# Which engine turns the normalised activations: K-tiles 8 to 15 on VectorE and through DRAM in place of TensorE

## The chip, the cores and the metric

The kernel runs on one core of one Trainium2 chip. It is a single launch, and its time is the device time of that launch in microseconds (us), given as the median of several runs. The engines that matter are TensorE (PE in the profile; its weight loads are shown apart as PEld), VectorE (DVE), ScalarE (ACT) and SyncE (SP), whose queue issues nearly all DMAs, one after the other. GpSimd (POOL) does almost nothing here.

## The reference

Two decoder layers on one sequence of 512 tokens and width 2048, all in float32. Layer 0 is a differential attention, layer 1 a forgetting attention that reads keys, values and forget gates projected once from the output of layer 0. The place of the change is the seam between the two: the layer norm that ends layer 0 and the projection behind it.

```python
def layer_norm(x, g, b):
    mu = jnp.mean(xf, axis=-1, keepdims=True)
    var = jnp.mean(jnp.square(xf - mu), axis=-1, keepdims=True)
    return (xf - mu) * lax.rsqrt(var + EPS) * g + b
...
y = diff_attention(h, ...)                       # ends in  o @ w_out
x = layer_norm(DN_ALPHA * x + gate * y, ln_g[0], ln_b[0])
...
# shared_kv
hk = x * (1.0 + scale) + shift
kvf = hk @ w_kv                                  # 2048 -> 4096 + 16
...
# layer 1
h = x * (1.0 + scale) + shift                    # another scale and shift
proj = h @ w_q                                   # 2048 -> 4096
```

## The kernel before

**Arithmetic.** Every float32 product is done as three products of rounded parts: an operand is split into a high part (`Hh`, `whi`) and the rest (`Hl`, `wlo`), and `products` (lines 227 to 231) issues high x high, high x low and low x high into one PSUM bank. The left or right operand on the activations' side has to lie with the width of 2048 on the partitions, so it is kept as 16 K-tiles of 128 features x 512 tokens, `Hh[kt]` and `Hl[kt]`.

**Weights.** `WeightStream` (lines 73 to 162) loads weights by SP's queue into four stage tiles (`wst`); each is cast by ACT into `whi` (line 117), DVE takes the rest into `wlo` (line 118), three buffers each.

**The end of layer 0.** `out_projection(oA, 0, ...)` multiplies by `a_w_out` in four jobs of 512 columns (f = 0 to 3). In the last job the weights of the last five of eight K-pairs are held back (`hold=5`, line 1089), and then worked off token block by token block (b = 0 to 3, 128 tokens each), five bursts of six matmuls a block. So block 0 is finished first. Behind each block comes `evac` on DVE (lines 1075 to 1086): the gate, the residual and the statistics, and then `norm_a(b)` (lines 1123 to 1130): mean and reciprocal deviation by a chain of small DVE instructions, the first 1024 columns of `n[:, b]` normalised by ACT, the others by DVE, and one store of the 1 MB block to `n_dram`, which layer 1 reads for its residual. `norm_a(3)` is the last of them.

**Turning.** `n` holds tokens on the partitions. `build_half(s, half)` (lines 1132 to 1153) makes one unit, K-tiles 2s and 2s + 1 for the token blocks 2 x half and 2 x half + 1: four TensorE transposes (line 1140) into a PSUM bank `sc`, of which there are two; for each K-tile two ACT instructions that apply scale and shift, into `htmp2` and into `Hh` (lines 1148 and 1149); one DVE subtraction into `Hl` (line 1150); and a DVE copy of the turned bank back over the same columns of `n` (line 1153). From there `build_h` (lines 1174 to 1180) later makes the `Hh` and `Hl` of layer 1 with the other scale and shift.

**The joint.** The first job on `kv_w` (`vj[0]`, 512 of the value columns) does not go K-pair by K-pair over all tokens but in the order `lag` (lines 1156 to 1159), 16 units written as (half, s): (0,0) (0,1) (0,2) (0,3) (1,0) (1,1) (1,2), then (0,s) (1,s-1) for s = 4 to 7, then (1,7). Half 0 runs ahead since token blocks 2 and 3 are normalised later. A unit consumes 12 matmuls of 512 columns (lines 1254 to 1258). `build_next` makes the next unit in that order: two are made during the last block of `out_projection` (line 1171), then one in each step of the loop (lines 1245 to 1262) except step 2, so that from step 3 on a unit is built one step ahead of its matmuls. Behind each step of half 1 the weight stream goes one on. I number steps and units from 0.

The instructions are traced in the order of the code, and the framework then orders those of each engine by its own plan; `tc.keep_in_program_order` holds an instruction at its place in the code.

Of the kernel before, what the change touches and what calls it, by code (L numbers as in the profile page):

```python
# [10 lines left out]
F32 = mybir.dt.float32  # L11
F32R = mybir.dt.float32r
I32 = mybir.dt.int32
AF = mybir.ActivationFunctionType
ALU = mybir.AluOpType

P = 128
D = 2048
# [147 lines left out]
def tile_yoco(  # L166
# [23 lines left out]
    nc = tc.nc  # L190
    V, S, PE, G = nc.vector, nc.scalar, nc.tensor, nc.gpsimd
    PSUM = bass.MemoryType.PSUM

    x = x[0]
    out = out[0]
# [7 lines left out]
    dram = ctx.enter_context(tc.tile_pool(name="dram", bufs=1, space=bass.MemoryType.DRAM))  # L203

    n_dram = dram.tile([T, D], F32, name="n_dram")
# [5 lines left out]
    def acc_bank(name="acc"):  # L211
        return ps.tile([P, 512], F32, name=name, tag="acc", bufs=4)

    def sc_bank(name="sc"):
        return ps.tile([P, 512], F32, name=name, tag="sc", bufs=2)
# [7 lines left out]
    def split(hi, lo, src):  # L223
        S.copy(hi, src)
        V.tensor_tensor(lo, src, hi.bitcast(F32), op=ALU.subtract)

    def products(dst, lhs, rhs, start, stop):

        PE.matmul(dst, lhs[0], rhs[0], start=start, stop=False)  # L229
        PE.matmul(dst, lhs[0], rhs[1], start=False, stop=False)  # L230
        PE.matmul(dst, lhs[1], rhs[0], start=False, stop=stop)  # L231
# [9 lines left out]
        out=mask[:, 384:], in_=mask[:, 384:], compare_op=ALU.is_ge, fill=NEG, base=0, pattern=[[-1, P]],  # L241
# [85 lines left out]
    oA = [(f, Job(a_w_out, [(512 * f, 512)]), (0, 1, 2, 3)) for f in range(4)]  # L327
# [24 lines left out]
    Hh = [None] * KT  # L352
    Hl = [None] * KT

    def new_h(kt):
        Hh[kt] = hpool.tile([P, T], F32R, name="hh", tag="H")
        Hl[kt] = hpool.tile([P, T], F32R, name="hl", tag="H")
# [591 lines left out]
    def drain():  # L949
        while pieces:  # L950
            tick(0)
# [84 lines left out]
    def ktile(name):  # L1036
        return kpool.tile([P, T], F32, name=name, tag="K")


    def row_bcast(t, src):  # L1040
        nc.sync.dma_start(t, src.partition_broadcast(P))

    def moments(pool, stats, b):
        mv = pool.tile([P, 2], F32, name="mv", tag="mv", bufs=4)
        V.bn_aggr(mv, stats[:, b, :, :])
        ve = pool.tile([P, 1], F32, name="lve", tag="lve", bufs=4)
        rstd = pool.tile([P, 1], F32, name="lrstd", tag="lrstd", bufs=4)
        V.tensor_scalar(ve, mv[:, 1:2], EPS, None, op0=ALU.add)
        rsqrt(rstd, ve, 1, pool)
        return mv, rstd  # L1050

    def out_projection(jobs, layer, zp, opened, residual, norm, after_held=None):


        ready = {}

        def prepare(k):
            if k < len(jobs):
                ready[k] = residual(jobs[k][0], jobs[k][2])

        prepare(0)
        for k, (f, job, banks) in enumerate(jobs):
            if layer == 1:

                if k == 1:
                    for piece in later:
                        pieces.extend([None, None, piece])
                pieces.extend([None] * (8 if k > 1 else 0) + [lambda k=k: prepare(k + 1)])
            elif k:
                prepare(k)  # L1070
            res = ready[k]
            gate = ktile("gate")
            row_bcast(gate, gate_dram[layer][0, 512 * f : 512 * (f + 1)])

            def evac(b, acc, f=f, res=res, gate=gate):
                if f == 0 and b == 0:
                    drain()
                    opened()
                pool, z, stats = zp
                zs = z[:, b, 512 * f : 512 * (f + 1)]  # L1080
                tmp = pool.tile([P, 512], F32, name="ztmp", tag="htmp", bufs=2)
                V.tensor_tensor(tmp, acc, gate, op=ALU.mult)
                res(b, zs, tmp)
                V.bn_stats(stats[:, b, f, :], zs)
                if f == 3:
                    norm(b)

            last = k == len(jobs) - 1
            group(job, True, evac, banks, bg=1 if k == 0 and layer == 0 else 0, hold=(5, 6)[layer] if last else 0, after_held=after_held if last else None)

    nctx = ExitStack()
    zp = []

    ab = {}
# [18 lines left out]
    def fold(k, row):  # L1113
        nc.sync.dma_start(row[0 : 2 * KT, 0:P], mod_dram[k].rearrange("v (a p) -> (v a) p", p=P))
        pt = tr_bank()
        PE.transpose(pt[:, 0 : 2 * KT], row[0 : 2 * KT, 0:P], ident[0 : 2 * KT, 0 : 2 * KT])
        a1, b1 = cols(f"mod_a{k}"), cols(f"mod_b{k}")
        V.tensor_tensor(b1, pt[:, KT : 2 * KT], bncol, op=ALU.mult)
        V.tensor_tensor(b1, pt[:, 0:KT], b1, op=ALU.add)
        V.tensor_tensor(a1, pt[:, KT : 2 * KT], gcol, op=ALU.mult)  # L1120
        return a1, b1

    def norm_a(b):
        pool, n, stats = zp
        mv, rstd = moments(pool, stats, b)
        mr = pool.tile([P, 1], F32, name="mr", tag="mr", bufs=4)
        V.scalar_tensor_tensor(mr, mv[:, 0:1], -1.0, rstd, op0=ALU.mult, op1=ALU.mult)
        S.activation(n[:, b, 0:1024], n[:, b, 0:1024], AF.Identity, scale=rstd, bias=mr)
        V.tensor_scalar(n[:, b, 1024:], n[:, b, 1024:], mv[:, 0:1], rstd, op0=ALU.subtract, op1=ALU.mult)
        nc.sync.dma_start(n_dram[b * P : (b + 1) * P, :], n[:, b, :])  # L1130

    def build_half(s, half):

        pool, n, _ = zp
        px = sc_bank()
        hs = slice(256 * half, 256 * half + 256)
        for q in range(2):
            for b in range(2):
                src = n[:, 2 * half + b, (2 * s + q) * P : (2 * s + q + 1) * P]
                PE.transpose(px[:, q * 256 + b * P : q * 256 + (b + 1) * P], src, ident)  # L1140
        for q in range(2):
            kt = 2 * s + q
            if half == 0:
                new_h(kt)
            tmp = pool.tile([P, 256], F32, name="htmp2", tag="htmp2", bufs=2)
            pq = px[:, q * 256 : (q + 1) * 256]
            sc, sh = ab["kv"][0][:, kt : kt + 1], ab["kv"][1][:, kt : kt + 1]
            S.activation(tmp, pq, AF.Identity, scale=sc, bias=sh)
            S.activation(Hh[kt][:, hs], pq, AF.Identity, scale=sc, bias=sh)
            V.tensor_tensor(Hl[kt][:, hs], tmp, Hh[kt][:, hs].bitcast(F32), op=ALU.subtract)  # L1150

        place = n[:, 2 * half : 2 * half + 2, 2 * s * P : (2 * s + 2) * P].rearrange("p b (q t) -> p q b t", t=P)
        V.tensor_copy(place, px.rearrange("p (q b t) -> p q b t", q=2, b=2))
# [8 lines left out]
    def build_next(n=1):  # L1162
        for _ in range(n):
            unit = next(built, None)
            if unit:
                build_half(unit[1], unit[0])
# [1 line left out]
    pieces.extend(attention_a(A_HEADS - 1, 1))  # L1168
    pieces.append(lambda: split_og((14, 15)))
    pieces.append(lambda: ab.update(kv=fold(0, ktile("mrow"))))  # L1170
    out_projection(oA, 0, zp, open_n, residual_a, norm_a, lambda b, k: build_next() if b == 3 and k < 2 else None)
    npool, n, nstats = zp

    def build_h(kts, ab):
        for kt in kts:
            new_h(kt)
            tmp = npool.tile([P, T], F32, name="htmp", tag="htmp", bufs=2)
            nt = n[:, :, kt * P : (kt + 1) * P]
            V.tensor_scalar(tmp.rearrange("p (b t) -> p b t", t=P), nt, ab[0][:, kt : kt + 1], ab[1][:, kt : kt + 1], op0=ALU.mult, op1=ALU.add)
            split(Hh[kt], Hl[kt], tmp)  # L1180


# [59 lines left out]

    acc = [acc_bank() for _ in range(TB)]
    held = {}
    for i, (half, s) in enumerate(lag):
        if i != 2:
            build_next()
        if (half, s) == (0, 3):
            ws.step(lambda: kpool.tile([P, 512], F32R, name="held", tag="K"))
            ws.load(ws.done + ws.STAGES - 1)  # L1250
        if half == 0:
            held[s] = ws.get(vj[0], s, 0)
        hi, lo = held[s]
        for b in (2 * half, 2 * half + 1):
            bs = slice(b * P, (b + 1) * P)
            for kq in range(2):
                kt = 2 * s + kq
                products(acc[b], (Hh[kt][:, bs], Hl[kt][:, bs]), (hi[kq], lo[kq]), kt == 0, kt == KT - 1)
            if s == KT // 2 - 1:
                evac_v(0)(b, acc[b])  # L1260
        if half == 1:
            ws.advance(ws.where[id(vj[0]), s] + 4)
# [310 lines left out]
```

## Time and profile before

| what | value |
|---|---|
| median of 3 runs | 1947.01 us (1946.09 to 1948.02) |
| the profiled execution: its time | 1948.57 us |
| its span, first to last instruction | 1946.7 us |
| TensorE clock granted, mean | 0.998 |
| PE busy from 0 to 60 us, 60 to 960 us | 40.68, 898.93 us |
| PE busy from 960 to 1035 us | 74.56 us |
| PE busy from 1900 to 1946.7 us | 34.27 us |
| GpSimd busy, whole span | 2.2 us |

All times inside the execution are counted from the start of the span. A busy time is a sum of instruction durations with overlaps taken out, so it says that an engine was occupied, not that the work could not have been shorter; for that one looks at the starts of successive instructions. "Idle before, releaser" is the time an engine stood still ahead of an instruction, and what ended it.

### The profile page before, as it was taken

How to read it: one execution, taken by the hardware profiler on the slowest of the kernel's cores; microseconds unless marked ns; L12 is line 12 of the kernel's file. 1: busy time of each engine (PE TensorE's matmuls, PEld its weight loads, DVE VectorE, ACT ScalarE, POOL GpSimd, SP SyncE). 2: the span in 40 equal slices, each digit the busy share in tenths (PEclk: the TensorE clock that was granted, in tenths of full speed). 3: DMA queues.
4: the chain of work that ended last, by engine and by line, in shares of the span. 5: the costliest groups of instructions: out<-in, count | busy, mean ns of one | idle time of the engine just before them, and what ended most of it. 6: DMA issues, size and time to landing. Idle time of an engine off the chain costs nothing.

```text
span 1946.7 us, 25419 instructions
## 1 busy us (share of the span) xinstructions
PE 1913.4 (98%) x8945; PEld 1611.4 (83%) x8945; DVE 1345.4 (69%) x2375; ACT 704.8 (36%) x1204; POOL 2.2 (0%) x10
## 2 busy tenths in 40 slices
PE   6999999999999999999999999999999999999997
PEld 4888888888888878888889998888888888888886
DVE  7995678877787778643575756565566666696657
ACT  3333434323333325531273222224334344453123
POOL 0000000000000000000000000000000000000000
PEclk9999999999999999999999999999999999999999
DMA  9993566877878774353337867654355555557622
GB/s 336 382 325 93 162 221 205 255 252 235 256 236 262 227 247 157 121 168 98 130 122 235 290 200 231 224 184 130 110 152 151 151 153 158 146 161 228 193 93 102
DMA packets 311851, 378.75 MB, mean 195 GB/s; under 512 B 56838, under 2 KB 237340, under 8 KB 310956
## 3 DMA queue, kind: packets, MB, share of 16 engines
q1 hardware_dynamic: 308720, 372.90, 60.1%
q10 hardware_dynamic: 3004, 4.23, 0.6%
q8 instruction: 70, 1.15, 0.2%
q14 instruction: 57, 0.47, 0.1%
HBM read 346.94 MB, written 30.10 MB: 194 GB/s over the span
## 4 chain that ended last, share of the span: by engine, by line
PE 89%; DVE 5%; DMA 3%; issue 1%; ACT 1%; SPq 1%; DVEq 0%; ACTq 0%
PE acc L229 25%; PE acc L230 25%; PE acc L231 25%; PE acc L677 4%; PE sc L679 2%; PE o L229 1%; PE o L679 1%; PE o L231 1%; PE o L230 1%; PE sc L231 1%; PE sc L230 1%; PE sc L229 1%; DVE wlo L118 1%; DMA ms<-in_w_mod_dram 1%; DVE macc L457 1%
## 5 line engine op out<-in xcount | busy, mean ns | idle before, releaser
L118 DVE TENSOR_TENSOR wlo<-wst,whi 128x1024 fp32r<-128x1024 f32 (+2 forms) x298 | 351.3, 1179 | 326.0 <-ACT whi L117 320.3
L117 ACT CAST whi<-wst 128x1024 fp32r<-128x1024 f32 (+2 forms) x298 | 303.3, 1018 | 666.4 <-PE acc L231 321.8
L229 PE MATMUL acc<-hh,whi 128*128 128x512 f32 x1184 | 464.2, 392 | 0.8 <-DVE sg L774 0.8
L230 PE MATMUL acc<-hl,whi 128*128 128x512 f32 x1184 | 462.2, 390 | 0.0
L231 PE MATMUL acc<-hh,wlo 128*128 128x512 f32 x1184 | 461.8, 390 | 0.0
L229 PE MATMUL acc<-whi,hh 128*128 128x512 f32 (+1 forms) x1168 | 445.0, 381 | 0.0
L230 PE MATMUL acc<-wlo,hh 128*128 128x512 f32 (+1 forms) x1168 | 442.8, 379 | 0.3 <-DVE wlo L118 0.3
L231 PE MATMUL acc<-whi,hl 128*128 128x512 f32 (+1 forms) x1168 | 442.4, 379 | 0.0
L231 PEld LDWEIGHTS acc<-hh,wlo 128*128 128x128 f32 x1184 | 222.6, 188 | 47.3
L229 PEld LDWEIGHTS acc<-hh,whi 128*128 128x128 f32 x1184 | 222.7, 188 | 44.2 <-issue 1.8
L230 PEld LDWEIGHTS acc<-hl,whi 128*128 128x128 f32 x1184 | 222.8, 188 | 42.0
L231 PEld LDWEIGHTS acc<-whi,hl 128*128 128x128 f32 x1168 | 219.4, 188 | 35.7
L230 PEld LDWEIGHTS acc<-wlo,hh 128*128 128x128 f32 x1168 | 219.6, 188 | 34.2 <-DVE wlo L118 0.8
L229 PEld LDWEIGHTS acc<-whi,hh 128*128 128x128 f32 x1168 | 219.5, 188 | 34.1
L457 DVE SCALAR_TENSOR_TENSOR macc<-ms,cact,macc 128x1024 f32<-128x1024 f32 (+1 forms) x180 | 197.8, 1099 | 27.5 <-DMA ms<-in_kv_w_mod_dram 14.0
L568 DVE SCALAR_TENSOR_TENSOR sacc<-sms,cact,sacc 128x512 f32<-128x512 f32 x112 | 77.1, 746 | 4.8 <-DMA sms<-in_w_mod_dram 4.5
L804 ACT ACTIVATE e<-e,mn 128x128 f32<-128x128 f32 (+3 forms) x64 | 36.0, 563 | 102.6 <-DVE mn L800 100.3
L1375 ACT ACTIVATE eb<-eb,mnb 128x128 f32<-128x128 f32 (+1 forms) x64 | 36.0, 563 | 85.6 <-DVE mnb L1372 85.4
L677 PE MATMUL acc<-whi,hh 128*128 128x512 f32 x128 | 51.8, 408 | 0.0
L677 PE MATMUL acc<-wlo,hh 128*128 128x512 f32 x128 | 50.1, 392 | 0.8 <-DVE wlo L135 0.8
L126 ACT CAST whi<-wst 128x768 fp32r<-128x768 f32 (+1 forms) x30 | 28.3, 944 | 60.5 <-PE o L679 33.7
L677 PE MATMUL acc<-whi,hl 128*128 128x512 f32 x128 | 50.0, 390 | 0.0
(270 smaller groups left out, 1981.8 us busy)
## 6 DMA issues: line engine op xcount, KB each, us to landing
wst<-in_a_w_in_dram SPq DMA_DIRECT2D x237, 256.0 KB, 4.3
ms<-in_w_mod_dram SPq DMA_DIRECT2D x64, 512.0 KB, 4.5
ms<-in_kv_w_mod_dram SPq DMA_DIRECT2D x64, 512.0 KB, 4.3
sms<-in_w_mod_dram SPq DMA_DIRECT2D x56, 512.0 KB, 7.6
wst<-in_b_w_in_dram SPq DMA_DIRECT2D x112, 256.0 KB, 2.9
wst<-in_kv_w_dram SPq DMA_DIRECT2D x40, 512.0 KB, 3.7
wst<-in_a_w_out_dram SPq DMA_DIRECT2D x32, 512.0 KB, 3.7
msk<-in_w_mod_dram SPq DMA_DIRECT2D x64, 256.0 KB, 5.2
```

The costliest lines, as they stand in the source:

```text
L117: self.nc.scalar.copy(hi[:, :, :w], st[:, :, :w])
L118: self.nc.vector.tensor_tensor(lo[:, :, :w], st[:, :, :w], hi[:, :, :w].bitcast(F32), op=ALU.subtract)
L126: self.nc.scalar.copy(hi[:, :, : job.width], self.stage[self.done][:, :, : job.width])
L229: PE.matmul(dst, lhs[0], rhs[0], start=start, stop=False)
L230: PE.matmul(dst, lhs[0], rhs[1], start=False, stop=False)
L231: PE.matmul(dst, lhs[1], rhs[0], start=False, stop=stop)
L457: ins = V.scalar_tensor_tensor(acc, w, cact[:, kt : kt + 1], acc, op0=ALU.mult, op1=ALU.add)
L568: V.scalar_tensor_tensor(acc, w, sc, acc, op0=ALU.mult, op1=ALU.add)
L677: PE.matmul(bank(v, b), h[:, bs], w, start=start, stop=stop)
L679: PE.matmul(bank(v, b), w[:, bs], h, start=start, stop=stop)
L804: S.activation(e[:, :w], e[:, :w], AF.Exp, bias=mn, scale=-1.0, accum_out=rs)
L1375: S.activation(e[:, :w], e[:, :w], AF.Exp, bias=mn, scale=-1.0, accum_out=rs)
```

## The change

The units with s = 4 to 7, that is K-tiles 8 to 15 (columns 1024 to 2047 of `n`, two groups of 512 with f = 2 and f = 3), are no longer turned by TensorE.

- `turn_out(b, f)`: a DVE transpose of the 128 x 512 piece of `n`, which turns each 32 x 32 square, into a new tile `nturn` (three buffers), held in program order; then a 256 KB store into a DRAM tile.
- `bring(b, f)`: four loads of 64 KB from that DRAM tile back over the same piece of `n`, one for each group of 32 features; with them the squares come to the partitions where they belong.
- `far(kt, blocks)` is the view of such a piece that gives K-tile kt; `build_far` does the rest of a unit from it: the same four ACT instructions, now read from `n` in SBUF, and the same two DVE subtractions. There is no transpose, no PSUM bank and no copy.
- Where they stand: (0,2) and (0,3) are turned out during the held bursts of block 1, (1,2) and (1,3) during those of block 2, (2,2) at the end of `norm_a(3)`, (3,2), (2,3) and (3,3) in steps 2 to 4 of the loop. (0,2) and (1,2) are brought back during the held bursts of block 3, ahead of `norm_a(3)`; the others in steps 0, 1, 4, 5, 7 and 8.
- In `norm_a(3)` ACT's 1024 columns are done in two instructions of 512, and the store to `n_dram` in four.
- In step 8 two units are built, so from there on a unit is built two steps ahead.
- `build_h` reads K-tiles 8 to 15 through `far`.

```diff
-        S.activation(n[:, b, 0:1024], n[:, b, 0:1024], AF.Identity, scale=rstd, bias=mr)
+        cuts = (0, 1024) if b < 3 else (0, 512, 1024)
+        for f0, f1 in zip(cuts, cuts[1:]):
+            S.activation(n[:, b, f0:f1], n[:, b, f0:f1], AF.Identity, scale=rstd, bias=mr)
         V.tensor_scalar(n[:, b, 1024:], n[:, b, 1024:], mv[:, 0:1], rstd, op0=ALU.subtract, op1=ALU.mult)
-        nc.sync.dma_start(n_dram[b * P : (b + 1) * P, :], n[:, b, :])
+        cuts = (0, D) if b < 3 else (0, 512, 1024, 1536, D)
+        for f0, f1 in zip(cuts, cuts[1:]):
+            nc.sync.dma_start(n_dram[b * P : (b + 1) * P, f0:f1], n[:, b, f0:f1])
+        if b == 3:
+            turn_out(2, 2)
+
+    sent = {}
+
+    def turn_out(b, f):
+        pool, n, _ = zp
+        t = pool.tile([P, 512], F32, name="nturn", tag="nturn", bufs=3)
+        src = n[:, b, 512 * f : 512 * f + 512]
+        ins = V.transpose(t.rearrange("p (a q c) -> p q a c", a=4, q=4), src.rearrange("p (q a c) -> p q a c", q=4, a=4))
+        tc.keep_in_program_order(ins)
+        sent[b, f] = dram.tile([P, 512], F32, name="turned_n", tag="turned_n", bufs=8)
+        nc.sync.dma_start(sent[b, f], t)
+
+    def bring(b, f):
+        to = zp[1][:, b, 512 * f : 512 * f + 512]
+        src = sent[b, f].rearrange("(m c) (a x) -> a c m x", m=4, a=4)
+        for a in range(4):
+            nc.sync.dma_start(to[32 * a : 32 * a + 32, :].rearrange("c (m x) -> c m x", m=4), src[a])
+
+    def far(kt, blocks):
+        f, q = divmod(kt, 4)
+        return zp[1][:, blocks, 512 * f : 512 * f + 512].rearrange("p b (m q c) -> p q b m c", m=4, q=4)[:, q]
+
+    def build_far(s, half):
+        pool = zp[0]
+        hs = slice(256 * half, 256 * half + 256)
+        for kt in (2 * s, 2 * s + 1):
+            if half == 0:
+                new_h(kt)
+            src = far(kt, slice(2 * half, 2 * half + 2))
+            tmp = pool.tile([P, 256], F32, name="htmp2", tag="htmp2", bufs=2)
+            sc, sh = ab["kv"][0][:, kt : kt + 1], ab["kv"][1][:, kt : kt + 1]
+            for out in (tmp, Hh[kt][:, hs]):
+                S.activation(out.rearrange("p (b m c) -> p b m c", b=2, m=4), src, AF.Identity, scale=sc, bias=sh)
+            V.tensor_tensor(Hl[kt][:, hs], tmp, Hh[kt][:, hs].bitcast(F32), op=ALU.subtract)
 
     def build_half(s, half):
-
+        if s >= 4:
+            return build_far(s, half)
...
-    out_projection(oA, 0, zp, open_n, residual_a, norm_a, lambda b, k: build_next() if b == 3 and k < 2 else None)
+
+    def between(b, k):
+        if b == 3 and k < 2:
+            build_next()
+        if b in (1, 2) and k in (2, 3):
+            turn_out(b - 1, k)
+        if b == 3 and k in (2, 3):
+            bring(k - 2, 2)
+
+    out_projection(oA, 0, zp, open_n, residual_a, norm_a, between)
...
-            nt = n[:, :, kt * P : (kt + 1) * P]
-            V.tensor_scalar(tmp.rearrange("p (b t) -> p b t", t=P), nt, ab[0][:, kt : kt + 1], ab[1][:, kt : kt + 1], op0=ALU.mult, op1=ALU.add)
+            if kt < 8:
+                to, nt = tmp.rearrange("p (b t) -> p b t", t=P), n[:, :, kt * P : (kt + 1) * P]
+            else:
+                to, nt = tmp.rearrange("p (b m c) -> p b m c", b=4, m=4), far(kt, slice(0, 4))
+            V.tensor_scalar(to, nt, ab[0][:, kt : kt + 1], ab[1][:, kt : kt + 1], op0=ALU.mult, op1=ALU.add)
...
+    brings = {0: (0, 3), 1: (1, 3), 4: (2, 2), 5: (3, 2), 7: (2, 3), 8: (3, 3)}
     for i, (half, s) in enumerate(lag):
         if i != 2:
-            build_next()
+            build_next(1 + (i == 8))
+        if 2 <= i < 5:
+            turn_out(*((3, 2), (2, 3), (3, 3))[i - 2])
+        if i in brings:
+            bring(*brings[i])
```

## The prediction

> **What bounds the kernel now.** The page first: its busy times and the chain that ended last.
>
> ```profile
> span 1946.7 us, 25419 instructions
> ...
> PE 1913.4 (98%) x8945; PEld 1611.4 (83%) x8945; DVE 1345.4 (69%) x2375; ACT 704.8 (36%) x1204; POOL 2.2 (0%) x10
> ...
> PE 89%; DVE 5%; DMA 3%; issue 1%; ACT 1%; SPq 1%; DVEq 0%; ACTq 0%
> ```
>
> TensorE is occupied for 98% of the span, and 89% of the chain runs over it. So time is gained where TensorE gets less to do or stops waiting, and work on other engines counts only where TensorE comes to wait for it. The stage that the change touches, cut into stretches (us, length, then busy time and count of PE, PEld, DVE, ACT, POOL, then clock and DMA share):
>
> ```profile
> 976.00:993.00 17.00, 17.00 (x85) 14.07 (x84) 16.39 (x47) 11.89 (x21) 0.00 (x0) 1.00 0.58 202
> 993.00:1003.00 10.00, 9.56 (x49) 7.48 (x48) 5.27 (x11) 7.80 (x15) 0.00 (x0) 1.00 0.26 108
> 1003.00:1034.00 31.00, 31.00 (x154) 25.56 (x153) 18.97 (x34) 23.33 (x44) 0.00 (x0) 1.00 0.27 81
> ```
>
> From 976 to 993 VectorE is as full as TensorE: 16.39 of 17 us. From 1003 on there is room on VectorE and ScalarE, and TensorE has no gap. The chain in order of time, and TensorE's own waits in this stage, say what happens at 993:
>
> ```profile
> 975.69 0.70 DVE ztmp L1082
> ...
> 992.69 1.25 ACT n L1128
> 993.99 0.55 PE sc L1140 x3
> ```
>
> ```profile
> PE sc L1140 <- ACT n L1128: 0.4, 1, 0.4
> ```
>
> The chain leaves TensorE at 975.69, goes along VectorE to the last norm, over its ACT instruction, and back to TensorE at 993.99: the transposes of unit 4 wait for block 3. That is the only wait of TensorE here.
>
> **What the transposes cost TensorE.** Durations overlap, so I go by starts. The timeline of TensorE:
>
> ```profile
> 989.64 0.39 PE L229 MATMUL acc<-whi,hh 128*128 128x512 f32 x1
> ...
> 992.36 0.27 PE L1140 MATMUL sc<-ident,n 128*128 128x128 f32 x1
> ```
>
> ```profile
> 1002.70 0.60 PE L1140 MATMUL sc<-ident,n 128*128 128x128 f32 x4
> 1003.05 0.48 PE L229 MATMUL acc<-whi,hh 128*128 128x512 f32 x1
> 1003.37 0.40 PE L230 MATMUL acc<-wlo,hh 128*128 128x512 f32 x1
> ...
> 1028.43 0.60 PE L1140 MATMUL sc<-ident,n 128*128 128x128 f32 x4
> ```
>
> From 989.64 to 992.36 lie the 12 matmuls of step 2, the one without transposes: 2.72 us, 0.227 us each. From 1002.70 (unit 7's transposes, step 6) to 1028.43 (unit 15's, step 14) lie eight steps of 12 matmuls and four transposes: 25.73 / 8 = 3.216 us each. So four transposes cost 0.50 us: 0.35 until the next matmul starts, some 0.09 in the first matmul (0.32 to the next start instead of 0.227), the rest in the matmuls behind. The change takes them from units 7 and 9 to 15, eight in all: **8 x 0.496 = 3.97 us off TensorE**, none of it hidden, since TensorE has no idle time there.
>
> The durations tell another sum. In the groups of this stage:
>
> ```profile
> L1149 ACT ACTIVATE hh<-sc,mod_b,mod_a 128x256 fp32r<-128x256 f32 x32 | 18.0, 564 | 0.0
> ...
> L1153 DVE COPY n<-sc 128x512 f32<-128x512 f32 x16 | 10.8, 682 | 0.0
> L1140 PE MATMUL sc<-ident,n 128*128 128x128 f32 x64 | 9.9, 274 | 0.4 <-ACT n L1128 0.4
> L118 DVE TENSOR_TENSOR wlo<-wst,whi 128x1024 fp32r<-128x1024 f32 x7 | 8.5, 1223 | 1.9 <-ACT whi L117 1.9
> ...
> L117 ACT CAST whi<-wst 128x1024 fp32r<-128x1024 f32 x7 | 7.2, 1052 | 4.8 <-PE acc L231 4.8
> ```
>
> 32 transposes of 274 ns would be 8.8 us; they overlap, so I don't take it. The Trainium skill (TensorE: Matmul & The Clock Gate, Part 4: PE-mode transpose) gives some 275 ns for a transpose inside a kernel; the trace agrees as to the duration, and by that rule, taken as a cost each, the sum would be the 8.8 us.
>
> **ScalarE in the far units.** Four instructions a unit stay, but read SBUF instead of PSUM. No row has this form. The nearest:
>
> ```profile
> L981 ACT ACTIVATE hh<-ogR,subg 128x256 fp32r<-128x256 f32 x28 | 19.6, 749 | 13.8 <-PE acc L230 13.8
> ...
> L1402 ACT CAST pTh<-pTl 128x256 fp32r<-128x256 f32 x16 | 6.4, 398 | 7.7 <-DMA pTl<-turned 7.7
> ...
> L1128 ACT ACTIVATE n<-n,mr,lrstd 128x1024 f32<-128x1024 f32 x4 | 5.0, 1248 | 13.1 <-DVE mr L1127 13.1
> ```
>
> ```profile
> 1012.99 0.56 ACT L1148 ACTIVATE htmp<-sc,mod_b,mod_a 128x256 f32<-128x256 f32 x1 [1.28 <-PE sc L1140]
> 1013.45 0.55 ACT L1149 ACTIVATE hh<-sc,mod_b,mod_a 128x256 fp32r<-128x256 f32 x1
> ```
>
> L1402 casts 256 columns from runs of 32, as `far` has them: 398 ns. Scale and bias from columns add 1248 - 1052 = 196 ns at 1024 columns. Together 0.594 us, an estimate; above lies L981, 749 ns, whose source jumps by four elements. Successive starts are 0.46 us apart at 0.56 us of duration, so each overlaps by 0.10. A unit then takes 4 x 0.494 = 1.98 us and half a weight cast of 0.95, in sum 2.45 us, below the 2.72 us that TensorE will need: cost nothing, with L981's value as a rival.
>
> **VectorE.** Off go eight copies of 0.682 us, all after 1000, where it had room: worth nothing. On come eight transposes:
>
> ```profile
> L911 DVE STREAM_TRANSPOSE e<-og 128x512 f32<-128x512 f32 x14 | 15.3, 1096 | 0.0
> ...
> L1386 DVE STREAM_TRANSPOSE tb<-eb 128x512 f32<-128x512 f32 x16 | 11.3, 708 | 0.3
> ```
>
> I take 0.71 us, for `turn_out` moves runs of 32 as L1386 does; L911, which scatters single elements, is the upper end. Four of them stand ahead of the norm of block 3. VectorE's idle time there:
>
> ```profile
> 968.89 0.69 DVE L1082 TENSOR_TENSOR ztmp<-acc,gate 128x512 f32<-128x512 f32 x1 [0.65 <-PE acc L231]
> ...
> 975.69 0.69 DVE L1082 TENSOR_TENSOR ztmp<-acc,gate 128x512 f32<-128x512 f32 x1 [1.52 <-PE acc L231]
> ...
> 995.69 0.42 DVE L1150 TENSOR_TENSOR hl<-htmp,hh 128x256 fp32r<-128x256 f32 x1 [2.30 <-ACT hh L1149]
> ```
>
> Two (1.42 us) fall into the 0.65 us ahead of block 1's work, which starts 0.77 late; two into the 1.52 us ahead of block 2's, which then start 0.77 late too and end 0.67 late. Between 976 and 993 VectorE has 0.61 us of idle time, of which part takes that up. So the last norm comes 0.1 to 0.7 us later, I take 0.5. Against it the split in `norm_a(3)`: unit 4 needs only the first 512 columns, which at 1248 ns for 1024 saves some 0.4 us. TensorE's wait at 993.99 stays: **+0.1 us**, bounds -0.4 (the wait gone) and +0.7. The four later transposes, 2.8 us, go into 993 to 1003, where 4.7 of 10 us are free; but the subtractions and copies for units 4 to 6 are in the same queue, and TensorE needs them at once: **+0.3 us**, between nothing and one transpose, 0.7.
>
> **SyncE and the DMAs.** Eight stores, 32 loads and three more pieces of `n_dram`. The way out and back of the same sizes and the same 512-byte runs stands in layer 0:
>
> ```profile
> L913 SPq DMA_DIRECT2D turned_rows<-e x14: 327/344/497, 249.7 to 777.3; - x14
> ...
> DMA to landing us min/median/max: 3.8/4.6/5.9
> ```
>
> ```profile
> L921 SPq DMA_DIRECT2D ogR<-turned_rows x56: 303/430/1487, 252.4 to 781.4; - x56
> ...
> DMA to landing us min/median/max: 1.9/3.8/6.7
> ```
>
> SP's own time: 11 x 0.34 + 32 x 0.43 = 17.5 us. SP is in order, and each load waits for its store's landing; behind it queue weight loads. The queue now:
>
> ```profile
> 1001.97 0.37 SPq L56 DMA_DIRECT2D wst<-in_kv_w_dram  x1
> 1005.24 0.37 SPq L56 DMA_DIRECT2D wst<-in_kv_w_dram  x1
> 1008.45 0.37 SPq L56 DMA_DIRECT2D wst<-in_kv_w_dram  x1
> 1021.31 0.37 SPq L56 DMA_DIRECT2D wst<-in_kv_w_dram  x1
> ```
>
> One trip: 0.71 + 0.34 + 4.6 + 4 x 0.43 + 3.8 = 11.2 us. The tightest is (3,2): turned about 995, back by some 1007 if it passes the load of 1001.97; unit 10 needs it on ScalarE at step 8 (1009) and on TensorE at step 10 (1014). It fits. (0,2) and (1,2) are out by 982 and have until 1002. A weight load a few us late has three other stages ahead of it. Cost nothing. The 4.2 MB more come while the DMA share is 0.26 to 0.27. In `build_h` (after 1300) DVE's reads have runs of 32 instead of 128; TensorE waits for none of them. The Trainium skill (VectorE: DVE Perf Modes, Rules for kernel authors) advises TensorE for a 128 x 128 transpose where PSUM will do, which speaks against the change; here the row of starts puts a price on that way.
>
> **Sum.** -3.97 + 0.1 + 0.3 = -3.6 us. The profiled execution took 1948.57 us, 1.87 beside its span, and would come to 1945.0; against the median, 1947.01, lower by 1.56 than that execution, it is **1943.4 us**. What follows the stage is TensorE-bound and moves up with it.
>
> **The rivals.**
> - VectorE's chain lengthens by all four transposes, since none finds its gap: 4 x 0.71 = 2.8 us instead of 0.5, which TensorE waits out at unit 4. For it: 16.39 of 17 us busy. Against: 2.17 us of idle time ahead. -3.6 + 2.3 = -1.3: 1945.7.
> - ScalarE becomes the bound, at 749 ns: 4 x 0.65 + 0.48 = 3.08 us a unit against 2.72, eight times 0.36 = 2.9 us. -0.7: 1946.3. Against: the row L1402 for the same run length.
> - Each transpose gives its full duration: -8.8 + 0.4: 1938.6. Against: the starts.
> - **Slower:** the plan puts the stores and loads of (2,3) and (3,3) behind the weight load that waited from 1008.45 to 1021.31. That load now issues about 1019.8. Loads alone behind it: 0.37 + 8 x 0.43 + 3.8 brings them in at 1027.4, ScalarE's 2.4 make it 1029.8, and TensorE wants unit 14 at 1028.43 - 7 x 0.5 = 1024.9: a wait of 4.9, 1948.3. Stores behind it too: 0.7 + 4.6 more, a wait of 10.2: **1953.6**. It decides where the last piece lands after about 1022.5. Against: in the code both stand ahead of that load. The Trainium skill (VectorE: DVE Perf Modes, The three transpose paths) warns that a strided DMA turns many times slower than the crossbar; here the runs are whole, and 3.8 us is measured.
>
> **How the numbers follow.** Forecast 0.62, VectorE's chain 0.12, ScalarE 0.09, full durations 0.04, SP with loads 0.05, SP with both 0.08. A measurement of this kernel can tell about 0.2%, 3.9 us, from no change, and the forecast lies just inside: its own bounds are -4.4 (all 3.97 and the wait of 0.4) and -2.6 (+0.7 twice). I give 0.36 of its 0.62 to more than 3.9: the wait at 993.99 may close, and the runs of before alone spread by some 1.0 to each side. Faster: 0.36 + 0.04 = 0.40; slower: 0.08; within: 0.52. The range runs from 1947.0 - 4.4 less 0.9 of that spread, 1941.7, to the loads-only case, 1948.3; outside are 0.12.
>
> **What would show it.** TensorE's starts: steps of 2.72 us from step 8 on. A wait of TensorE for `n` at unit 4 of 0.4 to 1.1 us. ScalarE's far instructions near 0.59 us. The last `bring` landed before 1020. Wrong would be any wait of TensorE for `hh` or `hl` after 1003, or a load of SP that stands behind a 12 us wait.

## The result and the profile after

The changed kernel takes 1942.45 us in the median of 12 runs, against 1947.23 us for the kernel before in 12 runs beside it. One of the 12 runs of the changed kernel took 4800.09 us, and the ratio leaves it out. The ratio is 0.9977, with a 95% interval of 0.9969 to 0.9985, that is 2.9 to 6.0 us less. The profiled execution took 1942.44 us.

The page of the changed kernel, its span, busy times and the chain that ended last:

```profile
span 1940.7 us, 25410 instructions
...
PE 1908.0 (98%) x8913; PEld 1607.8 (83%) x8913; DVE 1345.8 (69%) x2375; ACT 705.4 (36%) x1205; POOL 2.2 (0%) x10
...
PE 94%; DVE 3%; DMA 1%; ACT 0%; issue 0%; SPq 0%; DVEq 0%; ACTq 0%
```

TensorE has 32 instructions fewer. VectorE's sum is as it was, 1345.8 us: eight copies went and eight transposes came. The chain runs over TensorE for more of the span than before. The same stretches as in the prediction (the third ends earlier, as the stage does):

```profile
976.00:993.00 17.00, 16.28 (x80) 13.20 (x79) 16.45 (x47) 13.34 (x24) 0.00 (x0) 1.00 0.59 199
993.00:1003.00 10.00, 10.00 (x50) 8.26 (x49) 7.69 (x15) 8.44 (x17) 0.00 (x0) 1.00 0.87 285
1003.00:1030.00 27.00, 27.00 (x124) 22.55 (x123) 12.48 (x23) 22.46 (x42) 0.00 (x0) 1.00 0.51 152
```

VectorE is as full from 976 to 993 as it was. The copies that went off it had their place after 1000; of the transposes that came on it, four lie ahead of 976 (from 966.43 to 974.24) and four run from 991.73 on. The DMA share from 993 to 1003 is 0.87 where it was 0.26: there a large part of the way out and back runs. ScalarE is busy for 22.46 of the last 27 us. TensorE's only wait in the stage is the one that was there, and it is longer:

```profile
PE sc L1181 <- ACT n L1130: 0.7, 1, 0.7
```

**How long is the stage?** Since whole executions of one kernel differ by nearly as much as the change moves (those of the kernel before by up to 4.4 us), I take a length inside each profile: from unit 0's first transpose on TensorE to the first copy of a key tile on ScalarE, some 230 us later, where all of the first value job and what was planned into it is done. The rows of the two timelines, of before:

```profile
976.86 0.60 PE L1140 MATMUL sc<-ident,n 128*128 128x128 f32 x4
...
1211.15 0.59 ACT L1188 COPY kT<-acc 128x512 f32<-128x512 f32 x1 [0.53 <-PE acc L231]
```

and of after:

```profile
975.03 0.60 PE L1181 MATMUL sc<-ident,n 128*128 128x128 f32 x4
...
1205.56 0.59 ACT L1241 COPY kT<-acc 128x512 f32<-128x512 f32 x1 [0.53 <-PE acc L231]
```

1211.15 - 976.86 = 234.29 us, and 1205.56 - 975.03 = 230.53 us: **3.76 us less in the stage**. (The expectations below have 234.2 and 230.6, from starts rounded to a tenth.) The spans differ by some 6 us. Of that, 1.83 us lie ahead of the stage (976.86 against 975.03) and 0.3 us behind it. The 1.83 us are the run and not the change. The first instruction on any engine in which the two kernels differ is a VectorE transpose at 966.43, and TensorE is ahead by 1.82 us before that, when it comes to the held weights, though its instructions up to the stage stand in the same order in both kernels (the first row is of before, the second of after):

```profile
959.17 0.39 PE L229 MATMUL acc<-held,hh 128*128 128x512 f32 x1
```

```profile
957.35 0.39 PE L229 MATMUL acc<-held,hh 128*128 128x512 f32 x1
```

Over all profiles of this study the stage began anywhere from 974.6 to 978.0 us. From its end to the end of the span all of them take between 734.9 and 735.6 us, so what the change altered there, the reads of `build_h`, cost nothing that shows.

The end of the joint shows what a step costs now:

```profile
1003.80 0.60 PE L1181 MATMUL sc<-ident,n 128*128 128x128 f32 x4
1004.16 0.48 PE L229 MATMUL acc<-whi,hh 128*128 128x512 f32 x1
...
1028.77 0.34 PE L229 MATMUL acc<-whi,hh 128*128 128x388 f32 x1
```

After unit 8's transposes, the last there are, come steps 7 to 15, nine times 12 matmuls, until the next job begins with 388 columns: 1028.77 - 1004.16 = 24.61 us, 2.73 us a step, where it was 3.22.

### The profile page after: what moved, and what is told of

It reads as the page before. It is cut to its first block, busy times and chain, and to the rows that moved or that the text cites. A ratio compares the mean times of both kernels' runs of the same rounds, so it can differ in the third digit from the quotient of the medians.

```text
span 1940.7 us, 25410 instructions
## 1 busy us (share of the span) xinstructions
PE 1908.0 (98%) x8913; PEld 1607.8 (83%) x8913; DVE 1345.8 (69%) x2375; ACT 705.4 (36%) x1205; POOL 2.2 (0%) x10
## 4 chain that ended last, share of the span: by engine, by line
PE 94%; DVE 3%; DMA 1%; ACT 0%; issue 0%; SPq 0%; DVEq 0%; ACTq 0%
PE acc L229 27%; PE acc L230 27%; PE acc L231 27%; PE acc L677 4%; PE sc L679 2%; PE o L229 1%; PE sc L231 1%; PE o L231 1%; PE sc L230 1%; PE sc L229 1%; PE o L230 1%; PE o L679 1%; DMA sms<-in_w_mod_dram 1%; DVE sacc L568 1%; DVE wlo L118 0%; PE tr L603 0%
```

## The experiments

The theory to be tested (A): the gain is TensorE's issue time, 0.50 us for four transposes, eight times, less what VectorE's longer chain to the last norm costs. Against it: that the gain comes from what lies beside (no copy, no PSUM bank to wait for, the halved norm, the longer lead). "The stage" is the length defined above unless an expectation gives another; some of them use 57.50 and 53.74 us, the part of it up to the first matmul of 388 columns, which is shorter by the same 3.76 us. The kernels were measured in four groups, each with the kernel before beside it, so medians of different groups are compared with care and the stage decides.

| kernel | stage | median | before beside it |
|---|---|---|---|
| before | 234.29 | | 1947.5 to 1947.6 |
| changed kernel | 230.53 | 1942.45 | 1947.23 |
| changed kernel, once more | 230.56 | 1942.19 | 1947.54 |
| transposes kept as dummies | 234.46 | 1946.84 | 1947.52 |
| halved norm alone | 234.26 | 1947.39 | 1947.52 |
| without the lead | 230.54 | 1943.01 | 1947.52 |
| without the halved norm | 230.53 | 1943.71 | 1947.52 |
| K-tiles 12 to 15 alone | 232.39 | 1945.92 | 1947.59 |
| units 2 and 3 as well | 230.45 | 1943.09 | 1947.59 |
| four more VectorE transposes | 230.93 | 1944.10 | 1947.59 |
| last loads later in the code | 230.55 | 1943.66 | 1947.59 |
| (0,3), (1,3) turned after the last norm | 231.85 | 1945.24 | 1947.54 |
| both of these | 236.12 | 1949.45 | 1947.54 |

### The transposes put back as dummies

```diff
     def build_far(s, half):
         pool = zp[0]
+        px = sc_bank()
+        for k in range(4):
+            PE.transpose(px[:, k * P : (k + 1) * P], ident, ident)
```

> The changed kernel with four TensorE transposes of the identity put back into each far unit, into a PSUM bank that nothing reads. The stage from unit 0's first transpose to the first matmul of 388 columns was 57.50 us before and 53.74 us after. Theory A (what was gained is TensorE's issue time, 0.50 us for four transposes, eight times): the stage comes back to 57.5 to 57.8 us and the time to within 1 us of the kernel before. Rival B (the gain comes from the work beside it: no copy, no PSUM bank to wait for, ScalarE reading SBUF): the stage stays at 53.7 to 54.7 us, the time 4 to 5 us under the kernel before.

The rows that bound its stage:

```profile
977.04 0.60 PE L1184 MATMUL sc<-ident,n 128*128 128x128 f32 x4
...
1211.50 0.59 ACT L1244 COPY kT<-acc 128x512 f32<-128x512 f32 x1 [0.53 <-PE acc L231]
```

The stage is 234.46 us, the ratio to before 0.9997 (0.9988 to 1.0006): the whole gain is gone, though VectorE, ScalarE and the DMAs do all that the change gave them. The timeline of TensorE in that kernel:

```profile
1016.42 0.60 PE L1163 MATMUL sc<-ident 128*128 128x128 f32 x4
1016.77 0.48 PE L229 MATMUL acc<-whi,hh 128*128 128x512 f32 x1
1017.09 0.40 PE L230 MATMUL acc<-wlo,hh 128*128 128x512 f32 x1
```

The same 0.35 and 0.32 us as with the real ones. 53.74 became 57.67 us, 3.93 for 32 transposes, or 0.49 for four. Their durations would make 32 x 0.273 = 8.7 us. The Trainium skill (TensorE: Matmul & The Clock Gate, Part 4: PE-mode transpose) gives about 275 ns for a 128 x 128 transpose inside a kernel. The duration here, 0.273 us, agrees with it. What a transpose costs between matmuls is 0.12 us here, and the starts decide. Rival B falls.

### The halved norm alone, and the change without it

The first is the kernel before with the `cuts` of `norm_a(3)` and nothing else, the second the changed kernel with one instruction and one store there.

> The kernel before with only the last norm's ACT instruction in two halves and the last store in four; nothing is turned otherwise. Theory A: at most the wait at unit 4 goes, 0.6 us by starts; the stage is 56.9 to 57.5 us, the time 0 to 0.6 us under the kernel before. Rival B (the early half of the last norm is what pays): the stage is under 56 us.

> The changed kernel with the last norm's 1024 columns in one ACT instruction and the last store in one. Theory A: unit 4's transposes wait 0.3 to 0.45 us longer, the stage is 54.0 to 54.2 us. Rival D (the plan sets the transposes where it thinks their data come, so that the wait is the same): 53.7 us. Either way the time is within 0.5 us of the changed kernel's.

234.26 and 230.53 us: the halves are worth nothing either way, and rival D holds in the second. (Its median, 1943.71 us, is 1.3 above that of the changed kernel, where both theories had said 0.5 at most; the two were measured in different groups, and the stage shows no difference.) Why the halves are worth nothing is in the timelines of TensorE around unit 4's transposes, before:

```profile
992.36 0.27 PE L1140 MATMUL sc<-ident,n 128*128 128x128 f32 x1
992.39 0.47 PE L229 MATMUL acc<-held,hh 128*128 128x512 f32 x1
992.70 0.40 PE L230 MATMUL acc<-held,hh 128*128 128x512 f32 x1
992.93 0.39 PE L231 MATMUL acc<-held,hl 128*128 128x512 f32 x1
993.16 0.39 PE L229 MATMUL acc<-held,hh 128*128 128x512 f32 x1
993.99 0.55 PE L1140 MATMUL sc<-ident,n 128*128 128x128 f32 x3 [0.44 <-ACT n L1128]
```

and after:

```profile
990.54 0.27 PE L1181 MATMUL sc<-ident,n 128*128 128x128 f32 x1
990.56 0.47 PE L229 MATMUL acc<-held,hh 128*128 128x512 f32 x1
990.88 0.40 PE L230 MATMUL acc<-held,hh 128*128 128x512 f32 x1
991.99 0.55 PE L1181 MATMUL sc<-ident,n 128*128 128x128 f32 x3 [0.72 <-ACT n L1130]
```

Where half of the columns is normalised ahead of the other half, the framework's plan sets the three transposes behind two matmuls instead of four. The kernel before with the halves alone has two as well, the changed kernel without them four. TensorE then has less work issued ahead of the wait, so the wait grows though the data come a little earlier, 16.90 us after the stage's start instead of 17.08: from 993.16 to 993.99 it was 0.83 us for one matmul, from 990.88 to 991.99 it is 1.11.

### Without the longer lead

`build_next()` in step 8 in place of `build_next(1 + (i == 8))`.

> The changed kernel with one unit built in step 8 instead of two, so a unit is built one step ahead to the end. Theory A (ScalarE takes about 2.4 us for a far unit with its share of a weight cast, TensorE 2.72, so one step is enough): the stage stays at 53.7 us, give or take 0.2, and TensorE waits for nothing after unit 4. Rival C (the second step of lead covers ScalarE and the way back through DRAM): TensorE waits for hh or hl in the far units, 0.3 us or more in each of six, and the stage is 55.5 us or longer.

230.54 us, no wait of TensorE but the one at unit 4, ratio 0.9975 (0.9966 to 0.9984). One step of lead is enough; rival C falls. (By the measure that the expectation names this kernel shows 51.0 us, outside of A's range too. That is the measure and not a gain: the plan lets the next job begin, at 1026.78, ahead of the last unit's end, and the longer stage is as it was.) ScalarE's far instructions in the changed kernel:

```profile
L1169 ACT ACTIVATE hh<-n,mod_b,mod_a x16: 583/587/602, 988.7 to 1023.0; 128x256 fp32r<-128x256 f32 x16
L1169 ACT ACTIVATE htmp<-n,mod_b,mod_a x16: 585/590/611, 1000.8 to 1022.6; 128x256 f32<-128x256 f32 x16
```

```profile
1010.84 0.58 ACT L1169 ACTIVATE htmp<-n,mod_b,mod_a 128x256 f32<-128x256 f32 x1
1011.33 0.59 ACT L1169 ACTIVATE hh<-n,mod_b,mod_a 128x256 fp32r<-128x256 f32 x1
```

0.59 us and 0.49 us from start to start, as estimated.

### K-tiles 12 to 15 alone

`if s >= 6` in `build_half`, `kt < 12` in `build_h`, and no `turn_out` or `bring` with f = 2.

> The changed kernel with only K-tiles 12 to 15 (f = 3) turned by VectorE; K-tiles 8 to 11 go over TensorE again. Four groups of transposes off TensorE instead of eight. From unit 0's first transpose to ScalarE's first copy of a key tile it was 234.2 us before and 230.6 after; in this measure, theory A (0.50 us a group, VectorE's chain ahead of the last norm longer by at most 0.3): 232.2 to 232.6 us, the time 1.5 to 2.5 us under the kernel before. Rival E (the gain hangs on freeing the PSUM banks altogether, or comes in one piece): 230.6 or 234.2.

232.39 us: 1.9 us for four groups, half of the gain for half of the groups. With two transposes of VectorE fewer ahead of the last norm, TensorE's wait at unit 4 is 0.4 us as before the change. Rival E falls.

### Units 2 and 3 as well

```diff
-        if s >= 4:
+        if s >= 4 or (s >= 2 and half == 0):
             return build_far(s, half)
...
-        if b in (1, 2) and k in (2, 3):
+        if b in (1, 2) and k in (1, 2, 3):
             turn_out(b - 1, k)
-        if b == 3 and k in (2, 3):
-            bring(k - 2, 2)
+        if b == 3 and k in (1, 2):
+            bring(k - 1, 1)
+        if b == 3 and k in (3, 4):
+            bring(k - 3, 2)
```

> The changed kernel with units 2 and 3 (K-tiles 4 to 7 of token blocks 0 and 1) turned by VectorE too; for these K-tiles the later build for layer 1 takes two instructions instead of one. Theory A: two more groups off TensorE, -1.0 us; on VectorE two more transposes of 0.62 us ahead of the last norm, but two copies of 0.68 us less: the stage (to the first key copy) is 229.5 to 229.8 us, the time about 1 us under the changed kernel. Rival F (the way back is not done: block 1 is turned about 975, and units 2 and 3 are wanted from 987 on): ScalarE waits in its queue for the loads, TensorE waits for hh at units 2 and 3 and the last norm comes later; the stage is 231 us or longer.

230.45 us: the 1.0 us off TensorE came back nearly whole. TensorE's waits in this stage of that kernel:

```profile
PE acc L231 <- DVE lve L1048: 1.0, 1, 1.0
PE acc L231 <- DVE hl L1170: 0.2, 1, 0.2
```

Both are at matmuls that need an `hl` of unit 2, and the wait at unit 4 is gone; by starts the two lose some 1.6 us, where the wait at unit 4 lost 0.9 in the changed kernel. VectorE stood 0.64 and 0.59 us for ScalarE's half of the norm, since the K-tiles 4 to 7 lie in that half and the transposes are held at their place, so the work for block 2 began later, and the subtractions for unit 2 stood behind it in VectorE's queue: ScalarE had written the `hh` of its first K-tile by 987.35, and VectorE's subtraction began at 991.06. ScalarE stood only 0.6 us in all for loads. A's forecast failed, and F's cause is not what these rows show: they point to VectorE's queue, not to the loads. No run here sets the 0.6 us apart from the rest.

### Four more transposes on VectorE

```diff
             turn_out(b - 1, k)
+            more = zp[0].tile([P, 512], F32, name="more", tag="more", bufs=1)
+            tc.keep_in_program_order(V.transpose(more, zp[1][:, b - 1, 512 * k : 512 * k + 512]))
```

> The changed kernel with four more VectorE transposes of the same size, behind the four that stand in blocks 1 and 2, into a tile that nothing reads. Theory A (VectorE is full from 976 to 993, the chain to unit 4 runs over it; the first four mostly fell into gaps that are now used up): the wait at unit 4 grows from 0.7 by 2.2 to 2.5 us, the stage from 230.6 to 232.8 to 233.1 us. Rival G (VectorE still has room ahead of the last norm, the 0.3 us of the change came from elsewhere): 230.6 to 231.2 us.

230.93 us, within G's range and far from A's. 2.4 us of VectorE ahead of the last norm cost TensorE 0.4. But G's cause holds only in part: ScalarE's last norm begins 17.36 us after the stage's start, where the changed kernel has 16.09, so VectorE had room for about half of the 2.4. TensorE's wait changed its place:

```profile
PE sc L1181 <- DVE lrstd L303: 1.0, 1, 1.0
```

That is unit 2's transposes, in step 0. They need the bank of unit 0, which VectorE's copy frees, and that copy comes late (TensorE goes on at 983.28, and what the wait is put down to, `lrstd`, only ended last):

```profile
982.46 0.67 DVE L1194 COPY n<-sc 128x512 f32<-128x512 f32 x1
```

The wait at unit 4 is gone, though the last norm is later. The plan took two weight subtractions of VectorE, 1.2 us each, which in the changed kernel stand between the norm of block 2 and the work for block 3, forward into the norm of block 2, and set unit 4's transposes behind six matmuls instead of two. So "VectorE is full" in a stretch did not mean that every microsecond put on it is paid: part of what filled it could stand elsewhere, and TensorE had other matmuls to do.

### The last loads later in the code

```diff
-    brings = {0: (0, 3), 1: (1, 3), 4: (2, 2), 5: (3, 2), 7: (2, 3), 8: (3, 3)}
+    brings = {0: (0, 3), 1: (1, 3), 4: (2, 2), 5: (3, 2)}
...
             ws.advance(ws.where[id(vj[0]), s] + 4)
+        if i == 8:
+            bring(2, 3)
+            bring(3, 3)
```

> The changed kernel with the loads of (2,3) and (3,3) written behind the weight stream's advance of step 8 instead of ahead of it. Theory H (SP stands on that weight load for some 10 us, and what is queued behind it comes late): unit 14 waits for the loads, TensorE for 4 to 5 us; the stage is 234.5 to 236 us, the time back at that of before. Rival I (the framework's own plan orders SP's queue by when it thinks each DMA can start, so the place in the code counts little; or the landing is early enough): 230.6 us, no wait of TensorE.

230.55 us and no new wait. SP's queue in this kernel:

```profile
1003.35 1.46 SPq L56 DMA_DIRECT2D wst<-in_kv_w_dram  x3
1004.86 4.91 SPq L1153 DMA_DIRECT2D n<-turned_n  x8
1009.87 0.39 SPq L56 DMA_DIRECT2D wst<-in_kv_w_dram  x1
```

The eight loads go out at 1004.86, as they do in the changed kernel (1005.05), and ahead of the weight load that waits. Rival I holds: these loads, which have no fixed place, were ordered by the plan and not by the code. So this edit did not make them late: the slower case of the prediction was not set off, and what it would cost was not tried.

### (0,3) and (1,3) turned after the last norm

`turn_out(0, 3)` and `turn_out(1, 3)` in steps 3 and 4, (2,3) and (3,3) in steps 5 and 6, and their `bring`s in steps 6 to 8.

> The changed kernel with (0,3) and (1,3) turned in steps 3 and 4 of the loop, behind the last norm, instead of in blocks 1 and 2; their loads follow in steps 6 and 7. So two VectorE transposes (1.2 us) fewer stand ahead of the last norm. Theory J (what the wait at unit 4 loses goes back to where the plan sets unit 4's transposes and not to VectorE's load, as the run with four more transposes says, where 2.4 us cost 0.3): the stage is 230.4 to 230.7 us. Theory A as forecast (VectorE's chain is additive): the last norm comes 0.3 us earlier, the stage is 230.2 to 230.4 us.

231.85 us, worse than either. TensorE's waits in the stage:

```profile
PE acc L229 <- ACT hh L1169: 1.2, 1, 1.2
PE sc L1181 <- ACT n L1130: 0.4, 1, 0.4
```

The second line is what A said: two transposes fewer ahead of the norm, and the wait at unit 4 falls from 0.7 to 0.4 us. The first is new, at 1016.8 us, and ScalarE's timeline just ahead of it shows where it was:

```profile
1014.71 1.05 ACT L117 CAST whi<-wst 128x1024 fp32r<-128x1024 f32 x1 [3.58 <-PE acc L231]
1015.66 0.60 ACT L1169 ACTIVATE htmp<-n,mod_b,mod_a 128x256 f32<-128x256 f32 x1
```

A weight cast that can only start when TensorE is done with a buffer stands ahead of the far instructions, and ScalarE waits 3.58 us for it, with the unit that TensorE needs next behind it in the queue. In the changed kernel 15 far instructions stand between that cast and the one before it, here ten.

### Both of these

Units 2 and 3 far, f = 2 turned ahead of f = 1, and f = 3 after the last norm.

> Units 2 and 3 far as in the run that moved them, but (0,3) and (1,3) turned behind the last norm, and f = 2 turned ahead of f = 1 so that VectorE does not stand 0.6 us for ScalarE's half of the norm. VectorE has 2.5 us less ahead of units 2 and 3 than in that run, where TensorE waited 1.0 and 0.2 us for hl of units 2 and 3. Theory K (those waits were VectorE's load alone): they go, ten groups are off TensorE, the stage is 229.4 to 229.7 us and the time about 1 us under the changed kernel. Rival L (the loads of (1,1) come too late for unit 2 whatever VectorE does, since block 1 is turned only about 975): a wait of TensorE for units 2 and 3 stays, the stage is 230.2 us or more.

236.12 us and a ratio of 1.0011 (1.0003 to 1.0020): slower than before.

```profile
PE sc L1181 <- ACT n L1130: 3.0, 1, 3.0
PE acc L229 <- ACT hh L1169: 2.0, 2, 1.2
```

Unit 4's transposes, which need the last norm, now stand ahead of the matmuls of units 2 and 3 on TensorE, and ScalarE's instructions for unit 2 behind the last norm. ScalarE waits for no load in this stage: the cause that rival L names isn't what these rows show, though its forecast holds; K fell. No version was found that beats the change.

The changed kernel itself ran once more beside these two:

> The changed kernel once more, beside the two that follow, so that the three are compared on one chip. Both theories: the stage (from unit 0's first transpose to the first key copy) 230.6 us, the time 4 to 5 us under the kernel before.

Its stage is 230.56 us and its ratio 0.9976 (0.9967 to 0.9985), so the two kernels' losses are theirs and not the chip's. The gain in its median, 5.35 us, is a little more than the 4 to 5 expected.

## Why the prediction was right, point by point

- **3.97 us off TensorE.** Right: 3.93 by the dummies, 1.9 for half of the groups. The stage fell by 3.76 while the wait at unit 4 took 0.28 more by starts, which makes 4.04 for the real ones. The rival that counts each transpose by its full duration, 8.8 us, falls with it.
- **ScalarE at 0.594 us, its starts 0.49 apart.** Right, 0.59 and 0.49. The rival at 749 ns falls. The longer lead was not needed, as its run shows.
- **VectorE's chain, +0.1 us.** The terms were off. Two transposes in a row take 1.23 us from start to start of what follows, not 1.42:

```profile
966.43 1.31 DVE L1144 STREAM_TRANSPOSE nturn<-n 128x512 f32<-128x512 f32 x2
967.66 0.65 DVE L1082 TENSOR_TENSOR ztmp<-acc,gate 128x512 f32<-128x512 f32 x1
```

  ScalarE's last norm begins 16.09 us after the stage's start (991.12 against 975.03) where it was 15.83, so the chain grew by 0.26 us, not by 0.5. With two of the four transposes ahead of that norm left out, as in two of the runs, it is back at 15.83. The halved norm, counted at -0.4, brought nothing, as the plan moved the transposes ahead with it; the prediction took their place behind the matmuls as given. The wait at unit 4 went from 0.44 to 0.72 us, +0.3 in place of +0.1.
- **The four later transposes, +0.3 us.** They cost nothing: TensorE has no wait behind unit 4. The two terms were 0.4 us together and came out at 0.3, by errors that nearly cancel. So it is luck in these two terms that the sum of -3.6 us came within 0.2 of the stage's 3.76; the main term owes nothing to it.
- **SyncE and the DMAs at nothing.** Right for TensorE. The stores and the loads, as far as the trace records their landing:

```profile
L1147 SPq DMA_DIRECT2D turned_n<-nturn x8: 365/508/2163, 967.4 to 999.0; - x8
...
DMA to landing us min/median/max: 3.6/4.2/4.7
```

```profile
L1153 SPq DMA_DIRECT2D n<-turned_n x32: 302/430/1258, 973.1 to 1009.7; - x32
...
DMA to landing us min/median/max: 1.9/3.4/4.8
```

  The last load was issued at 1009.7, so it was in by some 1014.5 (an estimate, with the longest of these times), ahead of the 1022.5 from which I said that it would be late. One load is waited for, where the prediction saw time until 1002:

```profile
988.65 0.60 ACT L1169 ACTIVATE hh<-n,mod_b,mod_a 128x256 fp32r<-128x256 f32 x1 [0.84 <-DMA n<-turned_n]
```

  The plan set ScalarE's first far instruction ahead of the last norm. ScalarE stands 0.84 us for its load, but the norm's data are not there before 991.12, so TensorE loses nothing by it. The Trainium skill (VectorE: DVE Perf Modes, Rules for kernel authors) advises TensorE for a 128 x 128 transpose where a destination in PSUM will do. In this kernel, which TensorE bounds, taking half of them off it made the stage 3.76 us shorter.
- **The rival of VectorE's full chain** (2.8 us paid) is refuted as a price: 2.4 us more put the last norm off by 1.27 us and cost TensorE 0.4. As a mechanism it is there in a small size, 0.3 us for two transposes, seen when they were taken away.
- **The time.** 1943.4 us was forecast, 1942.45 measured. A gain of more than 3.9 us had a chance of 0.40, one within it 0.52: the medians lie beyond it with 4.8 us, though the stage's 3.76 alone would lie within. The 4.8 us between the medians are 1.0 more than the stage gives. That the stage alone moved is borne out only in part: the six runs (of the changed kernel and its variants) with a stage of 230.4 to 230.6 us have medians from 1942.2 to 1943.7, the two variants and the kernel before at 234.3 to 234.5 us from 1946.8 to 1947.6. The means are some 4.2 us apart, and the interval of 2.9 to 6.0 holds 3.76. Whether the rest is more than scatter is open.

## What to carry to other kernels

Price an instruction on a full engine by the starts around it, not by its duration: four transposes of 0.27 us cost 0.49 us between matmuls. The turn through DRAM was free here, since TensorE never came to wait for it. In the three variants in which TensorE waited for turned tiles it was not their landing that held it up but what stood ahead of their users in the queues of VectorE and ScalarE: look there first when such a change is widened. And where a framework plans the order, data that come earlier do not by themselves make the waiting shorter (0.18 us earlier, 0.28 us more of waiting here); look where the plan puts the waiting instruction.

## What the runs showed that I had not expected

Executions of kernels whose TensorE instructions up to there are in the same order reach the stage at 974.6 to 978.0 us, a spread nearly as large as the change. VectorE's transposes of 0.70 us start 0.6 us apart when they stand in a row. ScalarE takes 0.59 us for 128 x 256 with scale and bias from SBUF in runs of 32, hardly more than the 0.56 us from PSUM.
